# One PSUM layout for a whole block program: its last four banks become halves of two wide tiles, and the first recurrence head's queries are rounded in two parts

## The chip, the core and the metric

The kernel runs on one core of a Trainium2 chip. Its engines are TensorE (PE, matrix products), VectorE (DVE), ScalarE (ACT), GpSimd (POOL) and SyncE (SP, which issues most of the transfers). The metric is the device time of one launch in microseconds, lower is better.

## The reference, cut to what matters

Two transformer blocks follow each other on 512 tokens of width 1024, all in float32.

```python
def first_block(x, ...):
    h = h + token_mixer(rmsnorm(h, g_mix), ...)       # 4 differential heads and 8 sparse heads, one w_in, one w_out
    h = h + cross_attention(rmsnorm(h, g_xattn), rmsnorm(mem, g_mem), ...)
    h = h + conv_glu(rmsnorm(h, g_ffn), ...)          # width 2816
    return h

def dsa_attention(q, k, v, q_idx, k_idx, w_idx):      # the sparse heads
    score = einsum('bqh,bqhs->bqs', wib, relu(einsum('bqhd,bsd->bqhs', qib, k_idx)))
    _, idx = lax.top_k(score, topk)                   # 128 keys for each query
    ...                                               # softmax attention over the chosen keys

def diff_attention(q, k, v, lam):
    p = softmax(einsum('bqhcd,bshcd->bhcqs', qb, k) * D ** -0.5)
    a = p[:, :, 0] - lam * p[:, :, 1]
    return einsum('bhqs,bshe->bqhe', a, v)

def second_block(x, ...):
    y_a = hgrn2_branch(hq, hf, hi, hz, ...)           # a gated recurrence over chunks of 32 tokens, 8 heads
    y_b = mla_branch(cq, ckv, kr, mz, ...)            # latent attention, 8 heads
    x = x + (gates[:, :, 0] * (y_a @ w_proj_a) + gates[:, :, 1] * (y_b @ w_proj_b)) @ w_out
    return rms_norm(x, final_norm_g)
```

## The kernel before

**Products.** Every float32 value that goes into a product is held as a rounded high part and a low part. `hilo` makes them: ACT copies the value to the high part (L155), DVE subtracts it from the value for the low part (L156). A projection product is three matmuls, high by high, high by low, low by high (`mm3`, L224 to L226). Weights come by DMA into `WR0` to `WR2` and are converted by `split`, high part on ACT (L176) or POOL (L174) into the rings `WH0` to `WH3`, low part on DVE (L182) or by another DMA into `WL0` to `WL3`. Transposes are matmuls with an identity (`tr`, L452, and `trr`, L456).

**Stages.** In order of time: the input projections in chunks of 256 columns (to about 152 us); the index scores (L818) and top-k rounds (L835, L838); the differential heads in two halves `df0` and `df1`, each with units for four query blocks of two heads; the sparse heads (`dsa`); keys and values of the memory (`mem`); cross attention; the gated feed-forward; the second block's latent attention (`Mla`, about 870 to 1053 us); the recurrence with heads 0 to 7; the last projections.

**PSUM.** Before the recurrence PSUM is a pool `pp` of eight tiles `PS0` to `PS7` of 128 x 512 float32, one bank each. `banks(lin, sc, tr, out)` deals them to four rings: `plin` for projections, `psc` for attention scores, `ptr` for transposes, `pout` for the products with the values. In the index stage `psc` is `PS4`, `PS5`. In `df0` it is `PS0`, `PS4`, with `ptr` = `PS5`, `PS6` and `pout` = `PS7`. In `df1` and `dsa` `psc` is `PS2`, `PS3`, `ptr` is `PS4`, `PS5`, and two `pout` rings hold `PS6` and `PS7`. In cross attention and `Mla` `psc` is `PS3`, `PS4`, `ptr` is `PS5`, `PS6`, `pout` is `PS7`. Before the recurrence the pool is closed and a second one is opened over the same space: four tiles `PT0` to `PT3` of 512 columns and a ring `pairs` of two tiles `PU0`, `PU1` of 1024 columns.

**A unit of a differential head.** Scores of two score maps go into two `psc` tiles (six matmuls, L232). DVE masks each and finds its row extreme (`soft`, L626, with a read of the accumulator), ACT takes the exponential (L628), DVE forms the difference of the two maps (L632, L690, L691). The result is transposed into a `ptr` tile (L452), split by `hilo`, and multiplied by the values into the `pout` tile (L713 to L717). The last transposes of a block end in L731 and `hilo` again.

**Order.** The program is written as interleaved pipelines: in `df0` each step of a unit is followed by a step of `proj`, the projections that are left, so the projections fill PE while a unit waits for DVE and ACT. The program is built with the scheduler that models a timeline, so the order on each engine is the scheduler's own. It orders accesses to a PSUM tile by the tile.

**The recurrence's queries.** `Head.query` fills `F0` with 4 x 352 = 1408 columns and rounds them by one `hilo` into `X` (`R2` or `R3`) and `Y` (`R4` or `R5`). Heads 0, 2, 4, 6 use `R2`, `R4`, the others `R3`, `R5`. `Head.scores` multiplies them into the two `pairs` tiles.

Of the kernel before, what the change touches and what calls it, by code (L numbers as in the profile page):

```python
# [11 lines left out]
F32 = mybir.dt.float32  # L12
# [6 lines left out]
P = 128  # L19
# [44 lines left out]
def _body(nc, tc, ctx, d):  # L64
# [5 lines left out]
    PTS = nc.gpsimd.tensor_scalar  # L70

    cp = ctx.enter_context(tc.tile_pool(name="cp", bufs=1))
    banks_ctx = ctx.enter_context(ExitStack())
    pp = banks_ctx.enter_context(tc.tile_pool(name="pp", bufs=1, space=bass.MemoryType.PSUM))

# [5 lines left out]
    WH = [cp.tile([P, 1024], F32, name=f"WH{i}") for i in range(4)]  # L83
    WL = [cp.tile([P, 1024], F32, name=f"WL{i}") for i in range(4)]
    SMALL = cp.tile([P, 512], F32, name="SMALL")
    PS = [pp.tile([P, 512], F32, name=f"PS{i}") for i in range(8)]

    class Ring:
        def __init__(self, tiles):
# [9 lines left out]
    def sm(n):  # L99
        return smalls()[:, :n]  # L100

    wr_, wh_, wl_ = Ring(WR), Ring(WH), Ring(WL)
    plin, psc, ptr, pout = Ring(PS[0:3]), Ring(PS[3:5]), Ring(PS[5:7]), Ring(PS[7:8])

    def banks(lin, sc_, tr_, out_):

        o = 0
        for ring, n in ((plin, lin), (psc, sc_), (ptr, tr_), (pout, out_)):
            ring.t, ring.i = PS[o:o + n], 0
            o += n  # L110
        assert o <= 8

    def rr(ap):
        return ap.bitcast(F32R)
# [4 lines left out]
    def r3(ap, b):  # L119
        return ap.rearrange("p (a b) -> p a b", b=b)  # L120

    def f32(ap):
        return ap.bitcast(F32)
# [26 lines left out]
    def hilo(oh, ol, src, scale=None, pool=False):  # L150
        if pool:
            PTS(oh, src, scale, 0.0, op0=OP.mult, op1=OP.add)
            STT(ol, src, scale, f32(oh), op0=OP.mult, op1=OP.subtract)
        elif scale is None:
            ACT(oh, src, AF.Copy)  # L155
            TT(ol, src, f32(oh), op=OP.subtract)  # L156
        else:
            ACT(oh, src, AF.Copy, scale=scale)
            STT(ol, src, scale, f32(oh), op0=OP.mult, op1=OP.subtract)  # L159
# [4 lines left out]
    def setw(*m):  # L164

        wmode[:], wturn[0] = m, 0
# [84 lines left out]
    def lin_feat(X, w, c0, ps, ks=None):  # L251

        ks = list(range(X.nk)) if ks is None else ks
        for i, k in enumerate(ks):
            mm3(ps, w.h(k, c0, P), w.l(k, c0, P), X.hk(k), X.lk(k), i == 0, i == len(ks) - 1)
# [84 lines left out]
    for k in range(KD):  # L340
# [6 lines left out]
        c_ = slice((k % 2) * N0, (k % 2 + 1) * N0)  # L347
# [514 lines left out]
    banks(3, 2, 2, 1)  # L862
    plin.t, psc.t = PS[1:4], [PS[0], PS[4]]

# [284 lines left out]
    for half in range(2):  # L1149
        G = Act(11, R[0:3], R[3:6])  # L1150
        for i in range(11):
            f = half * 11 + i
# [21 lines left out]
        for j in range(KD):  # L1174
# [3 lines left out]
            t = sG()  # L1178
# [155 lines left out]
    PT = rr(R[6]).rearrange("p (j s c) -> p j s c", j=4, s=2)  # L1334
# [153 lines left out]


    setw("ad", "pd")  # L1490
    banks_ctx.close()
    p2 = ctx.enter_context(tc.tile_pool(name="p2", bufs=1, space=bass.MemoryType.PSUM))
    PS = [p2.tile([P, 512], F32, name=f"PT{i}") for i in range(4)]
    plin.t, ptr.t, pout.t = PS[0:2], PS[2:3], PS[3:4]
    pairs = Ring([p2.tile([P, 1024], F32, name=f"PU{i}") for i in range(2)])
    SC, RV, DS, E1 = S[0], S[1], S[9], S[15]
    nc.vector.memset(E1, 0.0)
    nc.vector.memset(r3(E1, 32)[:, :, 31:32], 1.0)
# [13 lines left out]
    NQ = 352  # L1512
# [3 lines left out]
    class Head:  # L1516
# [62 lines left out]
        def query(self):  # L1579
            w = W(d["w_hq"][self.h], KD, 128)  # L1580
            pc, dec, pre = self.pc, self.dec, self.pre
            ps = plin()
            lin_feat(X3, w, 0, ps)
            y, t = s1(), s1()
            TT(y, ps, rb3, op=OP.mult)
            ACT(t, y, AF.Tanh, scale=0.5)
            STT(t, t, 1.0, y, op0=OP.add, op1=OP.mult)


            f = F[0][:, 0:4 * NQ]  # L1590
            q = r3(f, NQ)
            own = q[:, :, 224:352]
            d4 = r3(dec, 4)
            STT(own, r3(t, P), 0.5, r3(pc, P), op0=OP.mult, op1=OP.mult)
            TT(q[:, :, 0:128].rearrange("p n (d c) -> p n d c", d=4), own.rearrange("p n (d c) -> p n d c", d=4),
               r3(pre, 4).unsqueeze(3).to_broadcast([P, NT, 4, 32]), op=OP.mult)
            for o, src, c in ((192, own[:, :, 96:128], 2), (128, own[:, :, 64:96], 1), (160, q[:, :, 192:224], 1)):
                PTT(q[:, :, o:o + 32], src, d4[:, :, c:c + 1].to_broadcast([P, NT, 32]), op=OP.mult)  # L1598
            hilo(self.X[:, 0:4 * NQ], self.Y[:, 0:4 * NQ], f)

        def keys_T(self):
            self.Z = Z = Zr(F32R)
# [167 lines left out]
    for n in range(NT):  # L1770
# [4 lines left out]
        t = sm(1)  # L1775
        for i, (c, o, m) in enumerate(pieces):
# [11 lines left out]
            else:  # L1788
                t0, t = t, sm(1)
# [88 lines left out]
```

## Time and profile before

| what | value |
|---|---|
| median of 3 runs | 1446.19 us (1444.57 to 1446.7) |
| profiled execution, its own time | 1444.99 us |
| its span from first to last instruction | 1443.2 us |
| mean granted TensorE clock | 0.994 of full speed |
| TensorE busy | 1416.9 us, 98% |
| VectorE busy | 941.3 us, 65% |
| ScalarE busy | 576.4 us, 40% |
| GpSimd busy | 424.2 us, 29% |

The span is the profile's; 1.8 us of the execution's time lie around it. A share of busy time is an average over stages, so a stage's own windows say which engine it waits for. The line numbers are those of the kernel before; in the changed kernel the same code stands one line lower up to the recurrence (L224 becomes L225, L452 becomes L453).

### The profile page before, as it was taken

To read this page: it belongs to the slowest core of one execution; us is meant where nothing else is said; L and a number is where in the kernel's file an instruction comes from. 1 tells how busy PE (TensorE), PEld (TensorE's weight loads), DVE (VectorE), ACT (ScalarE), POOL (GpSimd) and SP (SyncE) were. 2 spreads that over 40 slices of the span, in tenths; PEclk is the share of its full clock that TensorE was granted. 3 is DMA by queue.
4 is the path that set the end of the run, shared out by engine and by line. 5 is a ranking of instruction groups with operands and counts; after the bars stand their busy time and mean duration, and the time that the engine had idled before them with its cause. 6 is when DMAs were issued, how large, how long until landed. Compare 5 with 4: busy or idle time off the path is not lost.

```text
span 1443.2 us, 21066 instructions
## 1 busy us (share of the span) xinstructions
PE 1416.9 (98%) x7908; PEld 1229.7 (85%) x7908; DVE 941.3 (65%) x1819; ACT 576.4 (40%) x1171; POOL 424.2 (29%) x430
## 2 busy tenths in 40 slices
PE   8999999999999999999999999999999999999998
PEld 7999898888787888888888988888888899888887
DVE  8897898564546765366665455756438879785552
ACT  6766768545532222112233354444323332432211
POOL 4453215266332232223321202211114234321110
PEclk9999899999999999999999999999999999999999
DMA  7673353233122232332233333232442222266612
GB/s 232 149 165 85 90 161 109 80 123 107 50 88 86 90 93 83 103 117 88 92 89 103 103 130 95 92 110 91 139 135 67 90 93 75 81 197 219 195 54 88
DMA packets 58037, 160.01 MB, mean 111 GB/s; under 512 B 6224, under 2 KB 13904, under 8 KB 57936
## 3 DMA queue, kind: packets, MB, share of 16 engines
q1 hardware_dynamic: 55776, 151.33, 33.2%
q0 software_dynamic: 2016, 7.34, 2.9%
q8 instruction: 62, 1.02, 0.3%
q14 instruction: 39, 0.32, 0.1%
q10 hardware_dynamic: 144, 0.00, 0.0%
HBM read 142.92 MB, written 15.73 MB: 110 GB/s over the span
## 4 chain that ended last, share of the span: by engine, by line
PE 73%; DVE 3%; issue 3%; POOL 1%; ACT 1%; POOLq 0%; DVEq 0%; ACTq 0%
PE PS L225 16%; PE PS L224 16%; PE PS L226 16%; PE PT L224 7%; PE PT L226 7%; PE PT L225 7%; PE PS L452 1%; PE PS L1421 1%; DVE R L156 1%; DVE WL L182 0%; PE PT L452 0%; ACT R L155 0%; POOL F L1598 0%; DVE S L1547 0%; DVE Q L156 0%
## 5 line engine op out<-in xcount | busy, mean ns | idle before, releaser
L224 PE MATMUL PS<-R,WH 128*128 128x512 f32 x920 | 358.9, 392 | 1.7 <-DVE S L1172 1.0
L225 PE MATMUL PS<-R,WH 128*128 128x512 f32 x920 | 359.3, 391 | 0.2 <-DVE R L156 0.2
L226 PE MATMUL PS<-R,WL 128*128 128x512 f32 x920 | 358.1, 390 | 0.0
L182 DVE TENSOR_TENSOR WL<-WR,WH 128x1024 fp32r<-128x1024 f32 (+2 forms) x194 | 228.7, 1181 | 112.3 <-ACT WH L176 94.9
L176 ACT ACTIVATE WH<-WR 128x1024 fp32r<-128x1024 f32 (+1 forms) x140 | 147.7, 1056 | 228.8 <-PE PS L225 150.7
L224 PEld LDWEIGHTS PS<-R,WH 128*128 128x128 f32 x920 | 172.5, 188 | 37.4 <-DVE S L1172 1.5
L226 PEld LDWEIGHTS PS<-R,WL 128*128 128x128 f32 x920 | 172.7, 188 | 35.4
L225 PEld LDWEIGHTS PS<-R,WH 128*128 128x128 f32 x920 | 172.8, 188 | 34.8 <-DVE R L156 0.5
L174 POOL TENSOR_SCALAR WH<-WR 128x1024 fp32r<-128x1024 f32 (+4 forms) x92 | 92.8, 1008 | 361.9 <-PE PS L225 158.3
L224 PE MATMUL PS<-WH,R 128*128 128x256 f32 (+2 forms) x568 | 163.9, 294 | 6.7 <-POOL WH L174 6.7
L225 PE MATMUL PS<-WL,R 128*128 128x256 f32 (+2 forms) x568 | 166.0, 292 | 0.6 <-DVE WL L182 0.6
L226 PE MATMUL PS<-WH,R 128*128 128x256 f32 (+2 forms) x568 | 165.7, 292 | 0.0
L224 PE MATMUL PT<-R,WH 128*128 128x512 f32 x352 | 138.5, 394 | 0.3 <-DVE R L159 0.3
L226 PE MATMUL PT<-R,WL 128*128 128x512 f32 x352 | 137.5, 391 | 0.0
L225 PE MATMUL PT<-R,WH 128*128 128x512 f32 x352 | 137.5, 391 | 0.0
L224 PEld LDWEIGHTS PS<-WH,R 128*128 128x128 f32 x568 | 109.6, 193 | 9.5 <-POOL WH L174 6.7
L225 PEld LDWEIGHTS PS<-WL,R 128*128 128x128 f32 x568 | 109.6, 193 | 3.4 <-issue 1.4
L226 PEld LDWEIGHTS PS<-WH,R 128*128 128x128 f32 x568 | 109.5, 193 | 1.9 <-issue 0.7
L147 POOL TENSOR_TENSOR SMALL<-SMALL,nhalf 128x2 f32<-128x2 f32 (+3 forms) x43 | 47.5, 1109 | 122.6 <-DVE SMALL L1790 42.6
L224 PEld LDWEIGHTS PT<-R,WH 128*128 128x128 f32 x352 | 66.1, 188 | 13.9 <-DVE R L159 0.8
L226 PEld LDWEIGHTS PT<-R,WL 128*128 128x128 f32 x352 | 66.1, 188 | 13.8
L225 PEld LDWEIGHTS PT<-R,WH 128*128 128x128 f32 x352 | 66.1, 188 | 13.0
(402 smaller groups left out, 2587.2 us busy)
## 6 DMA issues: line engine op xcount, KB each, us to landing
WR<-w_fi_d SPq DMA_DIRECT2D x44, 512.0 KB, 3.7
WR<-w_inc_d SPq DMA_DIRECT2D x16, 512.0 KB, 6.8
WR<-w_fo_d SPq DMA_DIRECT2D x16, 512.0 KB, 3.7
WR<-w_gl_d SPq DMA_DIRECT2D x16, 512.0 KB, 3.5
WL<-w_inc_d POOLq DMA_DIRECT2D x14, 512.0 KB, 8.0
WR<-w_xk_d SPq DMA_DIRECT2D x8, 512.0 KB, 4.2
WR<-w_xv_d SPq DMA_DIRECT2D x8, 512.0 KB, 3.9
WR<-w_out_d SPq DMA_DIRECT2D x8, 512.0 KB, 3.8
```

The costliest lines, as they stand in the source:

```text
L147: PTT(out, x, nhalf[:, :n], op=OP.pow)
L156: TT(ol, src, f32(oh), op=OP.subtract)
L174: PTS(h, raw, 1.0, 0.0, op0=OP.mult, op1=OP.add)
L176: ACT(h, raw, AF.Copy)
L182: (TT if m[1] == "d" else PTT)(l, raw, f32(h), op=OP.subtract)
L224: nc.tensor.matmul(ps, sh, mh, start=first, stop=False)
L225: nc.tensor.matmul(ps, sh, ml, start=False, stop=False)
L226: nc.tensor.matmul(ps, sl, mh, start=False, stop=last)
L452: nc.tensor.transpose(out, in_, ident)
L1421: nc.tensor.matmul(ps, qp[hh][:, s_], rr(kpe[j])[:, :N], start=False, stop=j == 1)
```

## The change

There is one PSUM pool for the whole program: four tiles `PS0` to `PS3` of 512 columns and `PU0`, `PU1` of 1024. The names `PS[4]` to `PS[7]` are now views: `PS[4]` and `PS[5]` are the two halves of `PU0`, `PS[6]` and `PS[7]` those of `PU1`. `banks` deals them as before. No pool is closed before the recurrence; its rings take `PS0` to `PS3` and `PU0`, `PU1`. Head 0's queries are rounded in two `hilo` of 704 columns.

```diff
-    banks_ctx = ctx.enter_context(ExitStack())
-    pp = banks_ctx.enter_context(tc.tile_pool(name="pp", bufs=1, space=bass.MemoryType.PSUM))
+    pp = ctx.enter_context(tc.tile_pool(name="pp", bufs=1, space=bass.MemoryType.PSUM))
...
-    PS = [pp.tile([P, 512], F32, name=f"PS{i}") for i in range(8)]
+    PS = [pp.tile([P, 512], F32, name=f"PS{i}") for i in range(4)]
+    PU = [pp.tile([P, 1024], F32, name=f"PU{i}") for i in range(2)]
+    PS += [t[:, i * 512:i * 512 + 512] for t in PU for i in range(2)]
...
     setw("ad", "pd")
-    banks_ctx.close()
-    p2 = ctx.enter_context(tc.tile_pool(name="p2", bufs=1, space=bass.MemoryType.PSUM))
-    PS = [p2.tile([P, 512], F32, name=f"PT{i}") for i in range(4)]
     plin.t, ptr.t, pout.t = PS[0:2], PS[2:3], PS[3:4]
-    pairs = Ring([p2.tile([P, 1024], F32, name=f"PU{i}") for i in range(2)])
+    plin.i = 0
+    pairs = Ring(PU)
...
-            hilo(self.X[:, 0:4 * NQ], self.Y[:, 0:4 * NQ], f)
+
+            n = 2 if self.h == 0 else 1
+            for i in range(n):
+                c_ = slice(i * 4 * NQ // n, (i + 1) * 4 * NQ // n)
+                hilo(self.X[:, c_], self.Y[:, c_], f[:, c_])
```

The scheduler gives other orders on every engine. On PE they differ in the first third of the program and from the latent attention to the first recurrence head; the feed-forward stage and the later heads stand as before. In the built program 92 waits of PE are for an instruction that reads only the other half of the `PU` tile which the matmul writes; before, there is no such wait, since each bank was a tile of its own.

**Place A, PE, around the last projection matmul.** Before, the last three projection matmuls (on `WH3`, `WL3`), then a transpose of `df0`, the first scores of `df1` (128x512) and the first matmuls of the memory's keys (`WH0`):

```order
L224 MATMUL PS1_111<-WH3_104,R1_62 128x256
L225 MATMUL PS1_111<-WL3_108,R1_62 128x256
L226 MATMUL PS1_111<-WH3_104,R3_64 128x256
L452 MATMUL PS6_116<-cst_118,F0_73 128x128
L232 MATMUL PS2_112<-R7_68,R11_72 128x512
L232 MATMUL PS3_113<-R7_68,R11_72 128x512
L232 MATMUL PS2_112<-R7_68,R11_72 128x512
L232 MATMUL PS3_113<-R7_68,R11_72 128x512
L232 MATMUL PS2_112<-R7_68,R11_72 128x512
L232 MATMUL PS3_113<-R7_68,R11_72 128x512
L224 MATMUL PS0_110<-WH0_101,R2_63 128x256
L225 MATMUL PS0_110<-WL0_105,R2_63 128x256
```

After, the last ones stand among `df0`'s transposes and products with the values; behind them come more transposes (L453) and another unit's scores (L233 256 columns), with the waits shown:

```order
L226 MATMUL PS1_111<-WL3_108,R1_62 128x256
L227 MATMUL PS1_111<-WH3_104,R3_64 128x256
L715 MATMUL PU1_115<-R10_71,Q4_78 128x256 [waits DVE_49]
L718 MATMUL PU1_115<-R10_71,Q5_79 128x128
L714 MATMUL PU1_115<-R10_71,Q5_79 128x128
L715 MATMUL PU1_115<-R10_71,Q4_78 128x256
L714 MATMUL PU1_115<-R10_71,Q5_79 128x128
L715 MATMUL PU1_115<-R10_71,Q4_78 128x256
L453 MATMUL PU1_115<-cst_116,F0_73 128x128 [waits DVE_49]
L453 MATMUL PU1_115<-cst_116,F0_73 128x128 x3
L233 MATMUL PU0_114<-R8_69,R9_70 128x256 [waits DVE_49]
L233 MATMUL PS0_110<-R8_69,R9_70 128x256
```

Between the last projection matmul and the first matmul on `WH1` stood 61 matmuls; now it is 141 (16 of them, L947, are two each in the trace). Ahead of the last projection matmul stood 1073 and now 1013, so 60 have moved behind it; the other 20 stood behind the first matmul on `WH1`.

**Place B, VectorE, ahead of the conversion of the low weights `WL1`.** Before, the last rows of that stretch:

```order
L626 ISA S12_94,SMALL_109<-PS3_113,cst_118,keep_124 128x512
L626 ISA SMALL_109 128x1
L948 TENSOR_SCALAR keep_124<-PS4_114 128x2
L156 TENSOR_TENSOR R5_66<-PS5_115,R5_66 128x2x128
L731 TENSOR_SCALAR SMALL_109<-SMALL_109 128x1
L433 TENSOR_TENSOR S0_82<-S0_82,S2_84 128x512
L626 ISA S11_93,SMALL_109<-PS2_112,cst_118,keep_124 128x512
L626 ISA SMALL_109 128x1
L731 TENSOR_SCALAR SMALL_109<-SMALL_109 128x1
L950 TENSOR_SCALAR keep_124<-keep_124 128x2
L632 RECIPROCAL SMALL_109<-keep_124 128x1
L182 TENSOR_TENSOR WL1_106<-WR2_100,WH1_102 128x1024
```

After:

```order
L627 ISA SMALL_109 128x1
L633 RECIPROCAL SMALL_109<-keep_122 128x1
L627 ISA S13_95,SMALL_109<-PS2_112,cst_116,keep_122 128x512
L627 ISA SMALL_109 128x1
L157 TENSOR_TENSOR R5_66<-PU1_115,R5_66 128x2x128
L691 TENSOR_SCALAR SMALL_109<-SMALL_109,keep_122 128x1
L692 SCALAR_TENSOR_TENSOR S13_95<-S14_96,SMALL_109,S13_95 128x512
L949 TENSOR_SCALAR keep_122<-PU0_114 128x2
L951 TENSOR_SCALAR keep_122<-keep_122 128x2
L627 ISA S15_97,SMALL_109<-PS2_112,cst_116,keep_122 128x384
L627 ISA SMALL_109 128x1
L183 TENSOR_TENSOR WL1_106<-WR2_100,WH1_102 128x1024
```

Between the conversion of `WL3` and that of `WL1` stood 16 rows, and now 83. From the first softmax read (L627) behind the last projection matmul to the conversion of `WL1` there are 80 rows, which are 87 instructions (three rows stand for two, and four L839 have a load of their values that the order leaves out).

**Place C, PE, at the start of the recurrence.** Before, the last products of the latent attention with the values (`PS7`), then the recurrence's first projection (`PT0`):

```order
L224 MATMUL PS7_117<-R6_67,Q6_80 128x256
L225 MATMUL PS7_117<-R6_67,Q6_80 128x256
L226 MATMUL PS7_117<-R6_67,Q6_80 128x256
L224 MATMUL PS7_117<-R6_67,Q7_81 128x128
L225 MATMUL PS7_117<-R6_67,Q7_81 128x128
L226 MATMUL PS7_117<-R6_67,Q7_81 128x128
L224 MATMUL PT0_8553<-WH0_101,R8_69 128x256
L225 MATMUL PT0_8553<-WL0_105,R8_69 128x256
L226 MATMUL PT0_8553<-WH0_101,R10_71 128x256
L224 MATMUL PT0_8553<-WH0_101,R8_69 128x256
```

After, six of that projection's matmuls (now `PS0`) stand ahead of those products (now `PU1`):

```order
L227 MATMUL PS1_111<-R9_70,WL3_108 128x512
L225 MATMUL PS0_110<-WH0_101,R8_69 128x256
L226 MATMUL PS0_110<-WL0_105,R8_69 128x256
L227 MATMUL PS0_110<-WH0_101,R10_71 128x256
L225 MATMUL PS0_110<-WH0_101,R8_69 128x256
L226 MATMUL PS0_110<-WL0_105,R8_69 128x256
L227 MATMUL PS0_110<-WH0_101,R10_71 128x256
L225 MATMUL PU1_115<-R6_67,Q4_78 128x256
L226 MATMUL PU1_115<-R6_67,Q4_78 128x256
L227 MATMUL PU1_115<-R6_67,Q4_78 128x256
```

## Rows read from the trace of the kernel before

**Rows 1.** The page: the span, and busy time of each engine.

```profile
span 1443.2 us, 21066 instructions
...
PE 1416.9 (98%) x7908; PEld 1229.7 (85%) x7908; DVE 941.3 (65%) x1819; ACT 576.4 (40%) x1171; POOL 424.2 (29%) x430
```

**Rows 2.** Windows: stretch, its length, then PE, PEld, DVE, ACT, POOL busy, PEclk, DMA.

```profile
93.90:146.10 52.20, 52.20 (x402) 47.38 (x402) 43.49 (x127) 35.46 (x95) 19.09 (x20) 1.00 0.42 102
144.60:151.70 7.10, 7.10 (x64) 7.10 (x63) 5.14 (x17) 5.70 (x18) 2.29 (x2) 1.00 0.00 0
151.70:167.10 15.40, 13.22 (x80) 11.04 (x78) 11.09 (x30) 11.38 (x29) 6.75 (x7) 0.69 0.33 104
167.10:228.00 60.90, 60.89 (x485) 58.64 (x486) 57.92 (x154) 42.56 (x110) 12.26 (x18) 0.97 0.51 153
228.00:279.00 51.00, 48.61 (x319) 41.25 (x318) 37.53 (x114) 38.76 (x117) 19.55 (x26) 1.00 0.23 73
279.00:870.00 591.00, 586.91 (x2880) 494.13 (x2880) 332.77 (x460) 190.29 (x317) 190.09 (x156) 1.00 0.31 96
870.00:1052.90 182.90, 182.90 (x1017) 158.83 (x1016) 107.69 (x247) 76.28 (x172) 33.87 (x44) 1.00 0.35 110
```

**Rows 3.** Timeline of PE, 150 to 168 us: start, duration, instruction, idle before it.

```profile
151.44 0.28 PE L225 MATMUL PS<-WL,R 128*128 128x256 f32 x1
151.56 0.28 PE L226 MATMUL PS<-WH,R 128*128 128x256 f32 x1
...
156.39 0.54 PE L456 MATMUL PS<-identr,Q 128*128 128x128 f32 x4 [0.53 <-DVE Q L156]
...
162.99 0.75 PE L456 MATMUL PS<-identr,Q 128*128 128x128 f32 x4 [0.45 <-DVE R L156]
164.38 1.65 PE L232 MATMUL PS<-R,R 64*128 64x512 f32 x6 [0.64 <-DVE SMALL L626]
165.96 0.58 PE L224 MATMUL PS<-WH,R 128*128 128x256 f32 x1
167.11 0.58 PE L225 MATMUL PS<-WL,R 128*128 128x256 f32 x1 [0.58 <-DVE WL L182]
...
167.71 0.41 PE L224 MATMUL PS<-WH,R 128*128 128x256 f32 x1
167.92 0.41 PE L225 MATMUL PS<-WL,R 128*128 128x256 f32 x1
```

**Rows 4.** Timeline of DVE, 150 to 168 us.

```profile
156.32 1.22 DVE L182 TENSOR_TENSOR WL<-WR,WH 128x1024 fp32r<-128x1024 f32 x1
...
161.77 0.75 DVE L626 CUSTOM_DVE_ANT_0 S<-PS,cst,keep 128x512 f32<-128x512 f32 x1 [1.86 <-PE PS L452]
...
165.83 1.22 DVE L182 TENSOR_TENSOR WL<-WR,WH 128x1024 fp32r<-128x1024 f32 x1 [1.24 <-ACT WH L176]
```

**Rows 5.** Windows of 5 us over the same gap, columns as in rows 2.

```profile
155.00:160.00 5.00, 4.47 (x29) 4.28 (x29) 4.63 (x11) 3.58 (x8) 3.51 (x3) 0.74 0.23 66
160.00:165.00 5.00, 3.91 (x22) 3.44 (x24) 2.82 (x11) 2.41 (x9) 1.57 (x3) 0.50 0.71 224
165.00:170.00 5.00, 4.42 (x20) 3.48 (x17) 4.17 (x9) 4.13 (x9) 0.23 (x1) 0.50 0.43 123
170.00:175.00 5.00, 5.00 (x43) 5.00 (x42) 4.86 (x14) 3.81 (x9) 0.00 (x0) 0.89 0.37 115
```

**Rows 6.** Timeline of PE at the start of the recurrence.

```profile
1054.14 0.27 PE L226 MATMUL PS<-R,Q 128*128 128x128 f32 x1
1055.68 0.38 PE L224 MATMUL PT<-WH,R 128*128 128x256 f32 x1 [1.27 <-DVE S L1446]
...
1115.58 0.41 PE L224 MATMUL PU<-R 128*128 128x320 f32 x1 [0.43 <-ACT R L155]
1117.48 0.42 PE L225 MATMUL PU<-R,R 128*128 128x320 f32 x1 [1.49 <-DVE R L156]
```

**Rows 7.** Window over head 0's first scores, columns as in rows 2.

```profile
1090.00:1100.00 10.00, 10.00 (x51) 8.52 (x50) 8.59 (x9) 3.98 (x5) 4.99 (x6) 1.00 0.30 103
```

## The prediction

> **What bounds the kernel now.** I read the page first: TensorE is busy for 1416.9 of 1443.2 us [rows 1]. All PE idle time together is 26.3 us, so a change that leaves the matmuls as they are can gain little, and what it costs shows only where PE starts to wait. Then the windows by stage [rows 2]. While projections are left to fill in, PE has no gap (52.20 of 52.20 us and 7.10 of 7.10), though VectorE is already busy 43.49 of 52.20. From 151.7 to 167.1 us the filler is gone: PE is busy 13.22 of 15.40, at a mean granted clock of 0.69. After that PE is full again up to 228, loses 2.39 us up to 279, 4.1 in the 591 us behind, and nothing in the latent attention (182.90 of 182.90, VectorE 107.69). Third, the PE timeline over the one weak place [rows 3]. The last projection matmul starts at 151.56. Then PE waits several times for VectorE (0.53 for a low part, 0.45 for another, 0.64 for a softmax read), and the stretch ends when the low weights `WL1` are ready: L225 at 167.11 waits 0.58 for L182, which VectorE started at 165.83 and which takes 1.22 [rows 4]. So what ends this gap is the place of L182 in VectorE's order. Fourth, the start of the recurrence [rows 6]: 1.27 us for the closing of the old pool (released by L1446), and 0.43 and 1.49 for queries.
>
> **The change: what happens to the four last banks.** No matmul is added or taken. What moves is the order, because two banks that were separate tiles are now one. A matmul that writes `PS[4]` waits for the reader of `PS[5]`, and so on. In `df0` these are one score bank and a transpose bank (`PU0`), the other transpose bank and the output bank (`PU1`). A unit's scores then wait until VectorE has split the transposes in the other half, and transposes wait until the softmax has read the scores in the other half. Behind each such matmul the whole of PE's in-order queue stands, so the scheduler puts more projection matmuls ahead of it. They are spent earlier, and units of `df0` are left over. Place A shows it: 60 matmuls that stood ahead of the last projection matmul now stand behind it. At the mean of 52.20 / 402 = 0.130 us [rows 2] these are 7.8 us; most are transposes with shorter steps, and the steps of these 60 in the trace add up to 6.9. I take 7. The filler ends at about 151.7 - 7 = 144.7, if PE stays full until then.
>
> **Where the stall goes.** Behind the filler stand two units and a half of `df0`, the transposes of the sparse heads' queries, the first units of `df1` and the memory's statistics, and then `WH1`, which needs `WL1`. Its L182 now stands 80 rows, 87 instructions, behind the first softmax read (place B); before, 16 rows lay between `WL3` and `WL1`. VectorE's mean is 43.49 / 127 = 0.342 us [rows 2], so 87 x 0.342 = 29.8 us, and 1.22 for L182. The first of the 87 can start when the first scores are there, ten matmuls and six scores behind the filler: 144.7 + 1.5 = 146.2. The conversion ends at these times, depending on how much of the stretch VectorE is busy:
>
> - always: 146.2 + 29.8 + 1.2 = 177.2;
> - 0.95, as in 167.1 to 228 (57.92 of 60.90): 31.4 in place of 29.8, so 178.8;
> - 0.83, as in 93.9 to 146.1: 35.9, so 183.3;
> - 0.72, as in the gap before (11.09 of 15.40): 41.4, so 188.8.
>
> Before it ended at 165.83 + 1.22 = 167.05. The delay is 10.1, 11.8, 16.2 or 21.8 us. From that goes what PE does in the gap that it did behind it before: 20 matmuls x 0.130 = 2.6 (2.3 by their own steps). The net is 7.8, 9.5, 13.9 or 19.5. The stretch is a chain of scores, softmax, exponential on ACT, difference, transposes, split, in units that now take turns, so VectorE will wait a little, but it has four kinds of work to choose from. I take 12, between 0.95 and 0.83. PE has 141 matmuls there, about 18 us of work in 32 to 38 us.
>
> **The other places.** From 228 to 279 us `ptr` is `PU0` alone and the output banks are `PU1` alone, so transposes lose their second buffer; filler (the memory's keys) runs on into it. Idle time there is 2.39 now; I bound it by its all going and by its doubling, -2.4 to +2.4, and take +1. Cross attention and the latent attention pair a score bank with a transpose bank too; there a projection follows each step (PE 182.90 of 182.90), so I take 0, with +2.4 as a bound by the same row. The index stage has single score buffers now; the filler hides that, and its price is already in the 7 us. The first recurrence projection no longer waits for the closing (place C): six matmuls go ahead, -1.3, the 1.27 of rows 6.
>
> **The split queries.** The waits of 0.43 and 1.49 in rows 6 are head 1's: their operand is `R3`, which stays one piece. Head 0's queries fall where PE is busy 10.00 of 10.00 us [rows 7]; projections hide them. One more ACT and DVE instruction lies beside those. I take 0; without that cover, half of a 1408-column copy would be gained or its fixed cost lost, under 1 us.
>
> **Sum.** 12 + 1 + 0 - 1.3 = +11.7. The profiled execution's own time is 1444.99, so 1456.7. The median of the runs shown is 1.2 above that execution: 1458.
>
> **A rule against it.** The gap before shows what starving does to the clock: 0.74, 0.50, 0.50, 0.89 in four windows [rows 5], about 13.7 us at the lower level, 1.2 GHz, from 157.4 to 171.1. The fall came while PE waited again and again for VectorE, and projection matmuls behind it stepped by 0.21 in place of 0.12 us [rows 3]. The Trainium skill, "TensorE: Matmul & The Clock Gate", section "A second HAM failure mode: psum-queue depth-cycling", says that short idle times between groups of matmuls that cycle through banks can make the clock swing between its levels and cost throughput though each matmul looks right. By that rule this change, which shortens the cycle of banks, would bring further falls, and the third rival's time; by the rows alone only the one gap falls. The trace agrees as far as the one fall goes; it doesn't show a second.
>
> **Rivals.**
>
> - *The forecast*, +3 to +20: the gap grows, by VectorE's 87 instructions.
> - *The waits cost nothing*, the other side. If VectorE and ACT finish each half before PE comes to the other, the projections last as they did, and what is left is the start of the recurrence: 1.27, and if VectorE's head start also takes head 1's 0.43 and 1.49, 3.2 in all, so 1443. It decides only where the first third costs less than 0.3 us. For it speaks that PE was full up to 151.7 with VectorE at 0.83; against it that L182 stands behind 80 rows whatever the waits cost. The Trainium skill, "PSUM — Partial Sum Buffer", section "PSUM bank collisions raise a hardware error", says that accesses to different banks run clean and that waits are needed by bank; by that the waits between halves guard nothing and would not be there. The built order has them.
> - *The clock falls again*, in the longer gap and between 228 and 279, +20 to +35. A further stretch like the 13.7 us, filled with projections, does at 0.21 what takes 13.7 x 0.12 / 0.21 = 7.8 us, so it costs 5.9. One in the longer gap and one or two behind it give 12 + 6 to 18: about 1464 to 1476.
> - *The gap is mostly absorbed*, within 0.2%. If PE is not full up to 144.7, or the idle 2.4 and 4.1 us behind it shrink because work was done earlier, the loss may fall below 3: about 1447.
>
> **Chances.** Within 0.2% (2.9 us) is about what a measurement of this kernel can't tell from no change. The forecast 0.65; the clock 0.20; absorbed 0.09, of which a third lies just above the bound; the waits cost nothing 0.06. So slower 0.88, same 0.07, faster 0.05. The range reaches from +3 (the always-busy case with VectorE's mean 8% lower, 5.4, less 1.3 and 1) to +30 (19.5, 2.4 and 2.4 for the other places, 6 for one more fall), 1449 to 1476; the forecast's own is 1451 to 1465.
>
> **What would show it.** The last projection matmul near 145 us, L183 for `WL1` ending near 180 (before 167.05), PE busy some 20 of 35 us between them and a clock below 0.7; then everything behind it late by the same 9 to 14 us up to the recurrence; PE's wait for L1446 at the start of the recurrence gone; the waits of 0.43 and 1.49 still there. I am wrong if projections reach past 150 us, or if `WL1` is ready before 172. A time above 1468 would mean more falls of the clock than the one.

## The result, and the profile after

The changed kernel takes 1507.36 us (median of 4 runs, 1505.74 to 1508.2), the kernel before in the same runs 1445.38: a ratio of 1.0428, 95% interval 1.0416 to 1.0441. It is slower, as forecast, but by 62 us where 12 were forecast, far outside the range.

The page of the changed kernel, the span, busy time, and two of the lines of 40 slices:

```profile
span 1505.9 us, 21061 instructions
...
PE 1447.0 (96%) x7908; PEld 1247.0 (83%) x7908; DVE 946.9 (63%) x1820; ACT 583.4 (39%) x1172; POOL 426.0 (28%) x430
...
PE   8899699889999999999999999999999999999998
...
PEclk9999679999989999999999999999999999999999
```

PE does the same 7908 matmuls, yet it is busy 1447.0 us where it was 1416.9 [rows 1], 30.1 us more. Its idle time is 1505.9 - 1447.0 = 58.9 where it was 26.3: 32.6 more. The sum, 62.7, is the growth of the span. The lower clock does not explain all of the 30.1 us. The mean granted clocks of the two profiled executions (0.975, and 0.994 before) put about 75 us at the lower level, where it was about 17. At the steps seen below (0.21 in place of 0.12 us) the 58 us more cost about 25 us if PE was busy all through them, by my estimate, and less with its idle time. Among the rest are matmuls behind a wait, which overlap with no other: 0.58 us at 76.91, where the next one takes 0.41 at the same clock. In the slices the clock is lowest in the fifth and sixth (150 to 226 us, 6 and 7 tenths) and the ninth (301 to 339, 8 tenths).

Windows of the changed kernel, cut at the places where it loses time (columns as in rows 2):

```profile
70.90:76.90 6.00, 0.00 (x0) 0.00 (x0) 3.01 (x8) 2.93 (x6) 0.86 (x1) 0.68 0.91 199
153.30:202.00 48.70, 33.97 (x163) 27.22 (x161) 34.60 (x102) 28.67 (x84) 13.40 (x15) 0.59 0.11 33
159.08:200.61 41.53, 30.56 (x141) 24.76 (x141) 27.43 (x89) 22.88 (x74) 11.98 (x13) 0.54 0.10 31
159.08:192.73 33.65, 23.59 (x110) 18.65 (x111) 26.47 (x84) 21.79 (x72) 11.28 (x12) 0.55 0.03 13
255.00:334.00 79.00, 65.25 (x368) 51.60 (x367) 42.15 (x126) 45.42 (x132) 24.66 (x29) 0.94 0.20 63
427.00:460.00 33.00, 28.83 (x126) 22.49 (x125) 17.17 (x29) 13.98 (x31) 8.26 (x9) 0.84 0.10 33
460.00:1117.00 657.00, 654.22 (x3307) 555.35 (x3307) 380.47 (x612) 211.20 (x382) 162.72 (x156) 1.00 0.32 100
```

These stretches answer to those of [rows 2]. The gap that was 15.40 us (151.7 to 167.1) is now 48.70 (153.3 to 202.0), at a mean clock of 0.59 where it was 0.69. The stretch up to the first block's output projection, where 48.61 of 51.00 us were busy at full clock, now (255.0 to 334.0) has 13.75 us of idle time in 79.00 and a clock of 0.94. The end of cross attention (427 to 460) has lost 4.2 of 33 us and runs at 0.84. From there to the recurrence only 2.8 us of 657 are idle.

First, a wait that was not there, 80 us ahead of the gap. PE timeline of the changed kernel:

```profile
69.71 0.40 PE L819 MATMUL PU<-Q,R 128*128 128x256 f32 x2
...
70.41 0.39 PE L225 MATMUL PS<-WH,R 128*128 128x256 f32 x1
76.91 0.58 PE L226 MATMUL PS<-WL,R 128*128 128x256 f32 x1 [6.11 <-DMA WL<-w_inc_d]
77.29 0.41 PE L227 MATMUL PS<-WH,R 128*128 128x256 f32 x1
```

PE waits 6.11 us for low weights that POOL's queue brings. Behind the wait the projection matmuls step by 0.21 us, as at the lower clock in [rows 3]. Then the gap itself, PE (the last projection matmul is L227 at 153.17, the first on `WL1` L226 at 201.89):

```profile
153.17 0.28 PE L227 MATMUL PS<-WH,R 128*128 128x256 f32 x1
...
155.30 0.38 PE L233 MATMUL PU<-R,R 64*128 64x256 f32 x1 [0.72 <-DVE Q L157]
...
159.62 1.41 PE L233 MATMUL PS<-R,R 64*128 64x128 f32 x4 [2.50 <-DVE SMALL L627]
...
166.28 0.47 PE L233 MATMUL PS<-R,R 64*128 64x128 f32 x1 [1.49 <-DVE SMALL L627]
...
182.20 1.34 PE L457 MATMUL PU<-identr,Q 128*128 128x128 f32 x8 [2.25 <-DVE Q L566]
185.50 1.65 PE L233 MATMUL PS<-R,R 64*128 64x512 f32 x6 [1.96 <-DVE SMALL L627]
...
190.41 6.98 PE L948 MATMUL PU<-ones,WR 128*128 128x1 f32 x32 [1.08 <-ACT R L576]
...
201.89 0.58 PE L226 MATMUL PS<-WL,R 128*128 128x256 f32 x1 [0.36 <-DVE WL L183]
```

The longest of these waits are for VectorE: scores for the split of the transposes in the other half (0.72), scores for earlier softmax reads (2.50, 1.49, 1.96), transposes for the rotated queries (2.25, L566). In the whole gap PE waits 10.2 us for VectorE and 4.5 for ACT. The 32 matmuls of L948 (the memory's statistics) take 6.98 us without a wait between them, 0.22 each, at the lower clock. VectorE in the same stretch:

```profile
159.08 0.47 DVE L627 CUSTOM_DVE_ANT_0 F<-PS,cst,keep 128x256 f32<-128x256 f32 x1
...
170.04 0.35 DVE L627 CUSTOM_DVE_ANT_0 F<-PS,cst,keep 128x128 f32<-128x128 f32 x1 [0.56 <-PE PS L233]
...
179.18 0.69 DVE L434 TENSOR_TENSOR S<-S,S 128x512 f32<-128x512 f32 x1 [1.40 <-POOL S L432]
...
197.43 0.16 DVE L949 TENSOR_SCALAR keep<-PU 128x2 f32<-128x2 f32 x1 [4.70 <-PE PU L948]
...
200.61 1.23 DVE L183 TENSOR_TENSOR WL<-WR,WH 128x1024 fp32r<-128x1024 f32 x1 [1.30 <-ACT WH L177]
```

From the first softmax read, 159.08, to the conversion of `WL1`, 200.61, are 41.5 us, in which VectorE is busy 27.43 (window above). It is not the bound all through: it waits 0.56 for scores, 1.40 for POOL, 4.70 for the slow L948, and at the end 1.30 for ACT's high part of the weights (L177). What that ACT instruction waited for, what SyncE waited for before it issued the transfer (the list of its waits: total, number, longest), and the end of the gap in the chain that ended last (start, duration, what):

```profile
199.52 1.06 ACT L177 ACTIVATE WH<-WR 128x1024 fp32r<-128x1024 f32 x1 [7.88 <-DMA WR<-w_xk_d]
```

```profile
SPq L171 <- PE PU L948: 39.2, 2, 37.9
```

```profile
190.41 5.29 PE PU L948 x24
...
195.77 3.73 DMA WR<-w_xk_d
...
199.52 1.06 ACT WH L177
...
200.61 1.24 DVE WL L183
...
201.89 0.58 PE PS L226
```

So a transfer ends the gap, and SyncE stood 37.9 us for L948 before it could issue it. The weights for `WL1` (`w_xk`) go into the buffer that holds the memory's tokens until 24 of the 32 matmuls of L948 have read them, and L948 stands on PE behind the units that are left over. VectorE's last work ahead of this tail ends at 192.73. Up to there it is busy 26.47 of 33.65 us, a share of 0.79; in the 7.88 us up to L183 it mostly waits. Before, the same transfer was issued at 159.96, and ACT waited 0.82 for it:

```profile
159.96 0.33 SPq L170 DMA_DIRECT2D WR<-w_xk_d  x1
```

```profile
164.74 1.06 ACT L176 ACTIVATE WH<-WR 128x1024 fp32r<-128x1024 f32 x1 [0.82 <-DMA WR<-w_xk_d]
```

Behind, in the second differential half and the sparse heads, transposes alternate with their own split:

```profile
299.75 0.66 PE L453 MATMUL PU<-cst,F 128*128 128x128 f32 x4 [0.34 <-DVE Q L157]
...
301.82 1.12 PE L453 MATMUL PU<-cst,F 128*128 128x128 f32 x4 [0.34 <-DVE Q L157]
...
316.31 0.66 PE L453 MATMUL PU<-cst,S 128*128 128x128 f32 x4 [0.34 <-DVE Q L157]
```

Each time a transpose into one half of `PU0` waits 0.34 us for the low part (L157) of the transposes in the other half. Before, these were two tiles. The list of PE's waits puts them together, beside the two largest:

```profile
PE PS L226 <- DMA WL<-w_inc_d: 6.1, 1, 6.1
PE PS L233 <- DVE SMALL L627: 6.0, 3, 2.5
...
PE PU L453 <- DVE Q L157: 3.9, 11, 0.5
```

And the start of the recurrence, to hold against [rows 6]. The first matmul (L225 at 1117.05) waits for nothing now, head 1's queries are waited for as before:

```profile
1117.05 0.28 PE L225 MATMUL PS<-WH,R 128*128 128x256 f32 x1
```

```profile
1178.55 0.41 PE L225 MATMUL PU<-R 128*128 128x320 f32 x1 [0.72 <-ACT R L156]
1180.20 0.41 PE L226 MATMUL PU<-R,R 128*128 128x320 f32 x1 [1.25 <-DVE R L157]
```

### The profile page after: what moved, and what is told of

Its sections match the earlier page's. It is cut to its first block, busy times and chain, and to the rows that moved or that the text cites. A ratio compares the mean times of both kernels' runs of the same rounds, so it can differ in the third digit from the quotient of the medians.

```text
span 1505.9 us, 21061 instructions
## 1 busy us (share of the span) xinstructions
PE 1447.0 (96%) x7908; PEld 1247.0 (83%) x7908; DVE 946.9 (63%) x1820; ACT 583.4 (39%) x1172; POOL 426.0 (28%) x430
## 4 chain that ended last, share of the span: by engine, by line
PE 81%; DVE 8%; issue 3%; ACT 3%; DMA 3%; POOL 2%; SPq 0%; POOLq 0%; DVEq 0%; ACTq 0%
PE PS L225 24%; PE PS L226 24%; PE PS L227 24%; PE PU L453 3%; DVE WL L183 1%; DVE Q L157 1%; PE PU L226 1%; PE PU L227 1%; PE PU L225 1%; DVE R L157 1%; ACT Q L156 1%; DMA WR<-w_out_d 1%; DMA WL<-w_inc_d 0%; DVE S L296 0%; DMA S<-kv_d 0%
## 5 line engine op out<-in xcount | busy, mean ns | idle before, releaser
L225 PE MATMUL PS<-R,WH 128*128 128x512 f32 x1272 | 498.2, 393 | 3.0 <-DVE S L1173 1.0
L227 PE MATMUL PS<-R,WL 128*128 128x512 f32 x1272 | 497.4, 391 | 0.2
L226 PE MATMUL PS<-R,WH 128*128 128x512 f32 x1272 | 497.0, 391 | 0.2 <-DVE R L157 0.2
L183 DVE TENSOR_TENSOR WL<-WR,WH 128x1024 fp32r<-128x1024 f32 (+2 forms) x194 | 229.1, 1182 | 110.3 <-ACT WH L177 95.2
L225 PEld LDWEIGHTS PS<-R,WH 128*128 128x128 f32 x1272 | 238.9, 188 | 52.3 <-ACT R L156 1.9
L227 PEld LDWEIGHTS PS<-R,WL 128*128 128x128 f32 x1272 | 239.1, 188 | 49.6 <-DVE WL L183 0.6
L226 PEld LDWEIGHTS PS<-R,WH 128*128 128x128 f32 x1272 | 239.3, 188 | 48.2 <-DVE R L157 0.5
L177 ACT ACTIVATE WH<-WR 128x1024 fp32r<-128x1024 f32 (+1 forms) x140 | 147.6, 1055 | 239.9 <-PE PS L226 179.8
L226 PE MATMUL PS<-WL,R 128*128 128x256 f32 (+3 forms) x720 | 211.2, 294 | 7.0 <-DMA WL<-w_inc_d 6.1
L225 PE MATMUL PS<-WH,R 128*128 128x256 f32 (+3 forms) x720 | 211.0, 295 | 2.1 <-ACT F L423 1.1
L227 PE MATMUL PS<-WH,R 128*128 128x256 f32 (+3 forms) x720 | 210.2, 292 | 0.0
L226 PEld LDWEIGHTS PS<-WL,R 128*128 128x128 f32 x720 | 139.9, 194 | 10.4 <-DMA WL<-w_inc_d 6.3
L225 PEld LDWEIGHTS PS<-WH,R 128*128 128x128 f32 x720 | 140.2, 195 | 5.7 <-ACT F L423 1.4
L227 PEld LDWEIGHTS PS<-WH,R 128*128 128x128 f32 x720 | 139.9, 194 | 2.0 <-issue 0.4
L183 POOL TENSOR_TENSOR WL<-WR,WH 128x1024 fp32r<-128x1024 f32 x24 | 59.2, 2480 | 54.4 <-ACT WH L177 54.1
L156 ACT ACTIVATE R<-S 128x512 fp32r<-128x512 f32 x46 | 29.1, 632 | 109.9 <-DVE S L1173 44.5
L629 ACT ACTIVATE S<-S,SMALL 128x512 f32<-128x512 f32 (+3 forms) x75 | 42.2, 563 | 41.7 <-DVE SMALL L627 36.3
L453 PE MATMUL PU<-cst,S 128*128 128x128 f32 x272 | 49.0, 293 | 6.7 <-DVE Q L157 1.9
L453 PEld LDWEIGHTS PU<-cst,S 128*128 128x128 f32 x272 | 33.9, 148 | 15.9 <-DVE Q L157 2.8
```

The source lines that it names most:

```text
L177: ACT(h, raw, AF.Copy)
L183: (TT if m[1] == "d" else PTT)(l, raw, f32(h), op=OP.subtract)
L225: nc.tensor.matmul(ps, sh, mh, start=first, stop=False)
L226: nc.tensor.matmul(ps, sh, ml, start=False, stop=False)
L227: nc.tensor.matmul(ps, sl, mh, start=False, stop=last)
L453: nc.tensor.transpose(out, in_, ident)
```

## The experiments

Twelve kernels, and a thirteenth on what they left open. To see the places apart, I follow the start of four matmuls that are the same in every kernel: the first on `WL1` (167.11 in [rows 3]), the first of the first block's output projection (279.05), the end of cross attention's products (396.31), and the first of the recurrence (1055.68 in [rows 6]). The table gives the start in each kernel minus that before, in us, each from one profiled execution. Other work can move from one side of such a matmul to the other: in the changed kernel some 20 matmuls that stood behind the first one on `WL1` stand ahead of it.

| kernel | time | on `WL1` | output projection | end of cross attention | recurrence |
|---|---|---|---|---|---|
| after | 1507.36 | 34.8 | 54.7 | 62.9 | 61.4 |
| e1 layout alone | 1508.08 | 34.6 | 55.1 | 62.2 | 60.6 |
| e2 split alone | 1444.48 | -1.9 | -2.0 | -1.5 | -1.6 |
| e3 eight tiles | 1445.19 | -0.2 | -0.4 | 0.4 | -2.1 |
| e4 dealt across | 1504.17 | 30.9 | 38.7 | 47.9 | 55.6 |
| e5 first pair alone | 1491.7 | 21.4 | 38.0 | 45.2 | 46.7 |
| e6 second pair alone | 1469.94 | 5.3 | 18.4 | 18.6 | 22.6 |
| e7 second differential half freed | 1482.68 | 27.0 | 27.0 | 38.2 | 36.3 |
| e8 first differential half freed | 1492.26 | 13.3 | 39.0 | 46.1 | 44.6 |
| e9 all freed | 1528.22 | 17.6 | 16.5 | 44.5 | 74.7 |
| e10 freed from cross attention on | 1559.2 | 34.2 | 56.8 | 79.0 | 105.1 |
| e11 after, fewer top-k rounds | 1502.02 | 34.1 | 49.7 | 56.4 | 54.4 |
| e12 before, fewer top-k rounds | 1443.12 | -1.5 | -3.6 | -3.2 | -3.3 |
| e13 six banks | 1543.49 | 13.8 | 63.7 | 74.7 | 96.8 |

The times are medians, or the one run where there was one; the kernel before ran beside them at 1444.4 to 1445.2.

**e1: the layout alone.**

```diff
-            n = 2 if self.h == 0 else 1
+            n = 1
```

> The new layout with head 0's queries left in one piece. Theory (the halves): the query split hides behind projections, so the time is that of the changed kernel, 1507 us, within 2. Rival (the split disturbs the order of the recurrence's start): the time falls by some us below 1505.

1508.08 us (2 runs; ratio to before 1.0436, 1.0417 to 1.0455). The split has no part in the loss.

**e2: the split alone**, in the kernel before (the loop over two slices in place of the one `hilo`).

> The old two pools with head 0's queries in two pieces. Theory: 1445 to 1446 us, no change, since PE is busy all through those queries. Rival (the split gains or costs at the start of the recurrence): a change of more than 1.5 us.

1444.48 us, ratio 0.9997 (0.9988 to 1.0006): no change. The table's -1.6 is the difference of two single profiled executions, about what they spread.

**e3: eight tiles.**

```diff
-    PS = [pp.tile([P, 512], F32, name=f"PS{i}") for i in range(4)]
-    PU = [pp.tile([P, 1024], F32, name=f"PU{i}") for i in range(2)]
-    PS += [t[:, i * 512:i * 512 + 512] for t in PU for i in range(2)]
+    PS = [pp.tile([P, 512], F32, name=f"PS{i}") for i in range(8)]
...
-    pairs = Ring(PU)
+    pairs = Ring([PS[4:6], PS[6:8]])
...
-                nc.vector.copy_predicated(o, msk[:, 128:256].unsqueeze(1).to_broadcast([P, 2, P]), pa[:, :, 192:320])
+                for ii in range(2):
+                    oi, p = o[:, ii], pa[ii]
+                    nc.vector.copy_predicated(oi, msk[:, 128:256], p[:, 192:320])
```

(the three ScalarE copies likewise, once for each bank).

> One pool for the whole program, with eight separate tiles of one bank; the recurrence's pairs are two tiles each, worked bank by bank (six ScalarE copies and two VectorE copies where there were three and one); queries in two pieces. Theory (the halves do it all): the order of the first third is again that before, the loss of 62 us is gone, and the closing's 1.3 us is saved: 1443 to 1446 us. Rival (the single pool, open through the whole program, changes the scheduler's choices by itself): 1470 us or more.

1445.19 us, ratio 1.0002 (0.9993 to 1.0011): no change. The page:

```profile
span 1442.7 us, 21130 instructions
...
PE 1414.5 (98%) x7908; PEld 1227.2 (85%) x7908; DVE 939.4 (65%) x1836; ACT 583.5 (40%) x1220; POOL 424.4 (29%) x430
```

With the single pool and the split kept, but each bank a tile, the loss is gone, and the last input projection matmul starts at 151.99, where it was 151.56; in the changed kernel at 153.17. So all 62 us hang on the halves. At the recurrence e3 is 2.1 us early, the closing's 1.3 among them, but its span is only 0.5 us shorter (1442.7 and 1443.2): no gain in the time.

**e4: the halves dealt across**, so that `PS[4]` and `PS[6]` share a tile, and `PS[5]` and `PS[7]`.

```diff
-    PS += [t[:, i * 512:i * 512 + 512] for t in PU for i in range(2)]
+    PS += [t[:, i * 512:i * 512 + 512] for i in range(2) for t in PU]
```

> The changed kernel with the four halves dealt across: PS[4] and PS[6] are halves of the first tile, PS[5] and PS[7] of the second. The index scores and the transposes of the second differential half have two independent banks again; in the first differential half scores share a tile with a transpose bank, and the other transpose bank with the output bank. Theory (each ring that loses its second buffer pays in its own stage): the loss in the index stage (about 8 us) and between 228 and 279 us of before (22 us) goes, that of the gap stays: 1470 to 1485 us. Rival (any two halves shared cost the same, wherever): 1500 us or more.

1504.17 us, the rival's number. There is no 6 us wait for weights, and up to the output projection it is 16 us better, but from the end of cross attention to the recurrence, where nothing was lost, it now loses 7.7. My theory that each ring pays only for its own second buffer falls.

**e5 and e6: one pair at a time**, in the old two pools.

```diff
-    PS = [pp.tile([P, 512], F32, name=f"PS{i}") for i in range(8)]
+    PS = [pp.tile([P, 512], F32, name=f"PS{i}") for i in range(4)]
+    PW = pp.tile([P, 1024], F32, name="PW")
+    PS += [PW[:, 0:512], PW[:, 512:1024]]
+    PS += [pp.tile([P, 512], F32, name=f"PS{i}") for i in (6, 7)]
```

(e6: six single tiles first, then the two halves.)

> The old two pools; before the recurrence only PS[4] and PS[5] are halves of one tile, the other six banks are tiles of their own; queries in one piece. Theory (sharing score and transpose banks in the first differential half makes the gap): most of the loss, the index stage, the gap at 150 us and a part of 228 to 279: 1480 to 1498 us. Rival (the second pair costs as much): about half of the loss, 1470 to 1478 us.

> The old two pools; only PS[6] and PS[7] are halves of one tile. Theory (this pair couples transposes with the output bank in the first differential half, the two output banks between 228 and 279 us, and transposes with the output bank in cross attention): the 8 us of cross attention, some of 228 to 279, little of the gap: 1453 to 1468 us. Rival (the second pair costs as much as the first): 1470 to 1478 us.

1491.7 and 1469.94 us: +46.5 and +24.7, together 71, more than the 62 of both. The first pair makes most of the gap (21.4), most of what lies between it and the output projection (16.6) and nearly all of cross attention (7.2); the second pair has none of cross attention (0.2), against what I expected of it, but a loss of 13 ahead of the output projection and 4 from the end of cross attention to the recurrence. In e5 the last projection matmul starts at 145.84, as the forecast's 144.7 has it, and no wait for weights is there; in e6 there are two, 5.1 us in all:

```profile
PE PS L227 <- DMA WL<-w_inc_d: 5.1, 2, 3.6
```

So of the two pairs alone it is the second, which holds the index stage's transposes, that brings this wait. It takes more than the pair: e8 below deals the index stage as the changed kernel does, and there PE's score matmuls wait for ACT in its place.

**e7: scores and transposes on separate tiles in the second differential half**; **e8: the same in the first half only**.

```diff
-    poA, poB = Ring(pout.t[0:1]), Ring(pout.t[1:2])
+    psc.t, ptr.t, plin.t = PS[0:2], PS[2:4], [PS[4], PS[6]]
+    poA, poB = Ring([PS[5]]), Ring([PS[7]])
```

```diff
-    plin.t, psc.t = PS[1:4], [PS[0], PS[4]]
+    plin.t, psc.t = [PS[4], PS[6], PS[5]], PS[0:2]
+    ptr.t, pout.t = PS[2:4], [PS[7]]
```

> The changed kernel, but from the second differential half to the memory's keys the rings are dealt so that scores and transposes have the four separate tiles, and each projection bank shares a tile with an output bank. Theory A (228 to 279 us loses 22 us by its own shared halves): the 22 us go, about 1485 us. Theory B (that loss is inherited: the memory's projections were spent in the long gap, so none is left to fill in): at least 1500 us.

> The changed kernel, but in the first differential half scores and transposes have the four separate tiles, the projections take three halves and the output bank the fourth; the index stage before it and all stages behind it are as in the changed kernel. Theory: the last projection matmul comes late again, so the gap at 150 us is that of before and its 33 us are gone. Then theory A (228 to 279 us has its own loss): about 1475 us; theory B (inherited from the gap): about 1455 us.

e7: 1482.68 us. On `WL1` 7.8 us of the delay are gone (27.0): the memory's statistics, whose sums now go into a separate tile, stand early (from 155.57 us), the transfer of `w_xk` is issued at 159.94, and no transfer ends the gap. From `WL1` to the output projection nothing is lost (27.0 and 27.0; in the changed kernel 19.9): PE is busy 54.47 of the last 56.10 us and its clock is full:

```profile
250.00:306.10 56.10, 54.47 (x394) 49.17 (x393) 33.58 (x98) 41.47 (x116) 24.32 (x29) 1.00 0.32 101
```

e8: 1492.26 us. 13.3 us are left on `WL1`, where I expected none, and the loss behind it stays and is larger (25.7). Both say theory A: that stretch loses by its own shared halves, not by the long gap ahead. The 13 that e8 keeps come from the index stage, whose last score matmul starts at 84.1 us (before: 71.3); the last input projection is 11.4 late (162.91), so the gap itself is almost that of before. In the index stage each pair of scores now waits for the reading of the last:

```profile
PE PU L819 <- ACT S L821: 6.3, 7, 2.6
```

**e9: all rings dealt in that way up to the recurrence; e10: only from cross attention on.**

```diff
     O = Join(Oa, Ob)
     banks(3, 2, 2, 1)
+    plin.t, psc.t = [PS[4], PS[6], PS[5]], PS[0:2]
+    ptr.t, pout.t = PS[2:4], [PS[7]]
```

e9 has this, the edits of e7 and e8, and in the index stage:

```diff
     banks(4, 2, 2, 0)
+    plin.t, psc.t, ptr.t = [PS[4], PS[6], PS[5], PS[7]], PS[0:2], PS[2:4]
```

> The changed kernel's pool with its two wide tiles, but up to the recurrence the rings are dealt so that scores and transposes always have the four separate tiles, and projections and the output banks share the wide ones. Theory (a shared half costs only where the bank is held for a short time in turn with the other; a projection holds its bank for some microseconds, in which the other half is read): the loss is gone, 1443 to 1452 us. Rival (every shared half costs, whatever it holds): 1465 us or more.

> The changed kernel, but only from cross attention on the rings are dealt in that way. Theory: the delay up to 340 us is that of the changed kernel, and the 8 us of cross attention alone go: 1498 to 1502 us. Rival (those 8 us are inherited from the delay before): 1506 to 1509 us.

1528.22 (ratio 1.0575, 1.0558 to 1.0593) and 1559.2 us: slower still. My theory, as these rings are dealt, is wrong. e10's list of waits:

```profile
PE PU L225 <- DVE S L1160: 11.5, 13, 1.5
```

In a ring of `PU0`'s first half, `PU1`'s first half, `PU0`'s second half, the third and the next first bank are neighbours in one tile. The projection can't enter one before the other has been read: 13 waits of the feed-forward stage, up to 1.5 us each, stand bare on a PE that had next to none there (586.91 of 591 us busy, [rows 2]). So up to the output projection, where the ring has that neighbour only in the first differential half, e9 gains (16.5 late in place of 54.7), and from there to the recurrence it loses 58. It is the neighbour that costs, and not every projection bank on a shared half: in e7 each projection bank shares its tile with an output bank, and that stretch loses nothing.

**e11 and e12: fewer top-k rounds**, after and before. They leave out ten of the 16 rounds of the third query block and 15 of the fourth.

```diff
-            for _ in range(16):
+            for _ in range((0, 16, 6, 1)[b]):
```

> The changed kernel, leaving out top-k rounds of the later query blocks (6 of 16 and 1 of 16 are done). Theory V (VectorE's instructions bound the long gap one by one): the five rounds in the gap, 1.15 us each, are worth 5 to 7 us and more with the clock, 1494 to 1502 us. Theory L (the chain of scores, softmax, exponential, transposes bounds it, VectorE waits inside it): 1505 us or more.

> The kernel before, leaving out the same top-k rounds. Both theories: 1442 to 1446 us, since projections hide VectorE there and the short gap holds one round.

1502.02 and 1443.12 us. e11's time is in the range of theory V, but not at its place: the delay on `WL1` is 34.1, where it was 34.8, so five rounds less in VectorE's queue did nothing for the gap; the gain comes behind it. In the gap it is theory L: a chain through PE, VectorE, ACT and POOL with the weight transfer at its end, in which VectorE has room.

**e13: six banks.** Behind the first projection only one half of each wide tile is used. Between the two differential halves and the output projection the two output rings share one bank and overwrite each other's sums there.

```diff
     stream = first_units()
+    psc.t, ptr.t = [PS[4]], [PS[6]]
...
-    plin.t, psc.t = PS[1:4], [PS[0], PS[4]]
+    plin.t, psc.t = PS[1:3], [PS[0], PS[4]]
+    ptr.t, pout.t = [PS[3]], [PS[6]]
...
-    poA, poB = Ring(pout.t[0:1]), Ring(pout.t[1:2])
+    plin.t, psc.t, ptr.t = PS[0:2], PS[2:4], [PS[4]]
+    poA, poB = Ring([PS[6]]), Ring([PS[6]])
...
     O = Join(Oa, Ob)
     banks(3, 2, 2, 1)
+    plin.t, psc.t = PS[0:2], PS[2:3]
+    ptr.t, pout.t = PS[3:4], [PS[4]]
+    plin.t = plin.t + [PS[6]]
```

> The changed kernel with six banks dealt in place of eight: behind the first projection only one half of each wide tile is used before the recurrence, so no tile is shared by two rings, and each stage has two buffers less (one transpose bank, and one score or projection bank). Theory C (what costs is the coupling of two rings by one tile): giving the second halves up is faster than sharing them, below 1495 us. Theory N (a shared half is worth as much as none, what costs is the missing buffer): 1500 to 1515 us. Theory P (a shared half still helps as a buffer): above 1515 us.

1543.49 us: by the whole time, theory P. By place it differs: the first matmul on `WL1` is 13.8 late where sharing made it 34.8, so up to there a shared half is worse than none. In the second differential half (49.9 lost, though there the single output bank adds to it) and from cross attention to the recurrence (22) a shared half is much better than none. One execution shows this.

## Why the prediction was wrong

Right were the direction and the outline: waits between the halves, found in the built order, leave units of `df0` behind the filler, and the split has no share (e1, e2, e3). The closing's wait for L1446 is gone and head 1's waits are still there (0.72 and 1.25, where they were 0.43 and 1.49). From the end of cross attention to the recurrence nothing was lost (62.9 late, then 61.4 with the closing's gain). The forecast's +11.7 stands against 61.4 at the recurrence. One step had the wrong mechanism, what ends the gap; the other terms failed by size.

- *"The filler ends at about 144.7, if PE stays full until then."* It ended at 153.17, past the 150 that the text named as a sign of being wrong. PE was not full: it stood 6.11 us at 70.8 for a weight transfer, then ran at the lower clock for a while. I had put the index stage into the 7 us. In e5, which has no such wait, the 145.84 fits. That the scheduler used up converted weights sooner than transfers could bring new ones is my reading of the order; no run shows it by itself.
- *"So what ends this gap is the place of L182 in VectorE's order."* It is not. The row that I read this from [rows 4] has L182 wait 1.24 us for ACT, and ACT had waited for the transfer of `w_xk`, before and after. In the changed kernel that transfer could start only at 195.77, since L948 stood on PE behind the leftover units.
- *"I take 12, between 0.95 and 0.83."* With the 2.3 us of work that was brought forward this puts the end of the conversion at 181.3; it ended at 201.84, 20.5 later. The later end of the filler makes 8.5 of that. The first softmax read came 5.9 us behind the last projection matmul, where I had 1.5: 4.4 more. VectorE's own stretch was sized rightly (33.65 us up to 192.73, where the 12 allows 34.0). The last 7.9 are the tail of L948, transfer and ACT, for which the sum has no term. So the gap's 12 became 34.8, less the 2.3: 32.5. The nearness of those 34.0 and 33.65 us is partly luck: VectorE's share was 0.79, lower than the 0.83 to 0.95 of my choice, and its instructions were shorter than their mean.
- *"-2.4 to +2.4, and take +1"* for 228 to 279 us: from `WL1` to the output projection it is 19.9, and 22.2 with those 2.3 (e7 takes all of it away). I bounded it by the idle time already there, which says nothing of a wait that does not exist yet. The rows for it were PE's waits for a low part, 0.53 and 0.45 [rows 3], once for each transpose that lost its second buffer: the list has eleven such, and others behind them. Idle time grew there by 13.75 - 2.39 = 11.4 us; the clock has a share in the rest.
- *"so I take 0, with +2.4 as a bound"* for cross attention: 8.2, by the first pair (7.2 in e5, 0.2 in e6).
- *"by the rows alone only the one gap falls"*: the clock is up to about 25 of the 62.7 us, by the estimate above. It fell in the wait for weights (0.68 in that window), through the gap, in the second differential half and in cross attention, in the last three where PE waits some tenths of a microsecond again and again. The rival with more falls (0.20) was nearer, and its 1464 to 1476 was still too small, since it kept the 12 for the gap and counted no idle time behind it. The Trainium skill, "TensorE: Matmul & The Clock Gate", section "A second HAM failure mode: psum-queue depth-cycling", spoke against this change. The trace agrees: clocks of 0.59, 0.94 and 0.84 in the windows above where the banks cycle with fewer tiles. The Trainium skill, "PSUM — Partial Sum Buffer", section "PSUM bank collisions raise a hardware error", asks for waits by bank. e3, with one tile for each bank, has no more than those on these four banks, and it loses nothing; the waits by tile beyond them cost the 62 us.

The forecast's own range stands there twice, as +3 to +20 and as 1451 to 1465 (+5 to +19); nothing hangs on the difference.

How much of the loss is the waits on the chip and how much the order that the scheduler made from them, stays open: no run had the one without the other. Nor is it settled how much of the idle time comes from the lower clock itself, which stretches the chain.

## What to carry to other kernels

Where dependencies are kept by tile, a wide tile cut into views is one thing to wait for: two rings on its halves wait for each other. Prefer tiles of one bank, with the wide operation split in two, as in e3. When filler runs out, follow what ended the gap in the trace back to its first cause, through the conversion to the transfer and to the instruction that frees its buffer, and see where that instruction stands in the new order. Multiply a short wait by every place in the built order that gains it. Projections are no cover for a bank whose neighbour in the ring is in the same tile.

## What was not expected of the hardware

- The lower clock can strike the work behind the idle time and not the idle stretch. From 295 to 300 us PE was busy 3.02 of 5.00 at the full clock; from 300 to 305 it was busy 4.57, and the mean clock was 0.67. From 280 to 290 us the same: busy 3.52 at 0.97, then 5.00 at 0.69. It is no rule: in the 6 us without a matmul from 70.9 to 76.9 the mean clock was 0.68.

```profile
280.00:285.00 5.00, 3.52 (x21) 2.58 (x20) 2.65 (x10) 4.02 (x16) 0.70 (x1) 0.97 0.16 57
285.00:290.00 5.00, 5.00 (x23) 4.46 (x23) 2.03 (x8) 2.48 (x8) 1.86 (x4) 0.69 0.00 0
295.00:300.00 5.00, 3.02 (x15) 1.65 (x14) 2.93 (x11) 4.00 (x15) 3.41 (x5) 1.00 0.00 0
300.00:305.00 5.00, 4.57 (x23) 3.97 (x22) 2.73 (x6) 2.60 (x6) 0.00 (x0) 0.67 0.00 0
```

- A matmul of one column took as long as one of 256: 22 of the statistics' matmuls (128x1) took 2.56 us in e3 at the full clock, 0.12 each, which is the step of the 256-column projection matmuls.

```profile
157.32 2.56 PE L946 MATMUL PS<-ones,WR 128*128 128x1 f32 x22
```

- The two pairs alone cost 46.5 and 24.7 us, both together 62, so the price of one pair depends on the other. Why is not shown; each kernel has an order of its own.
